# Delta rule in a hybrid decoder trunk: joining 16-row blocks by products with 32x32 weights instead of masked 128x128 weights

## The chip, the cores and the metric

The kernel runs on one NeuronCore of a Trainium2 chip. The metric is the device time of one execution in microseconds (us), as the median of several runs. A profile is one execution of its own; its times are counted from the start of its span.

## The reference

A decoder trunk of 4 layers works on 256 positions of 1024 channels, in fp32. Layers 0 and 3 mix the positions by attention, layer 1 by a short convolution, layer 2 by the gated delta rule; a convolutional feed-forward block follows each mixer. The change is in the delta rule alone:

```python
a_mat = jnp.where(strict, jnp.einsum('bhnid,bhnjd->bhnij', k_beta, k) * decay, 0.0)
t_mat = lax.linalg.triangular_solve(a_mat + eye, eye, left_side=True, lower=True, unit_diagonal=True)
u = t_mat @ v_beta
w = t_mat @ (k_beta * jnp.exp(gc)[..., None])
```

So for each of the 8 heads, and each chunk of the sequence, the inverse of a lower triangular matrix with unit diagonal is needed. The kernel takes chunks of 128 positions, so there are 16 such matrices of 128x128.

## The kernel before, in words

**The work.** Nearly all of the time is products of a stream of fp32 weights with the activations. Each weight tile is split into a high part `whi` (line 152, ScalarE) and a low part `wlo` (line 153, VectorE), and each product is three matmuls. The weights come in chunks of 8 tiles, each by one DMA. All matmuls are recorded at line 254, all transposes at 257.

**The delta rule.** `gdn` (layer 2) runs the weight products of queries, keys, values and gates as a *fill* in a fixed order (`GDN_FILL`), and weaves the delta rule's own small steps between them. The 8 heads form two halves of 4: half 0 (heads 0 to 3) and half 1 (heads 4 to 7). The fill brings half 0's queries and keys first, so half 0 goes through each step first, though half 1 stands first in the planner's list. A half has 8 matrices (4 heads, 2 chunks). Its steps, in `half`:

- `lengths` and `systems` make the matrices `aq` (line 758). `systems` sends them to DRAM (line 766) and, in the kernel before, makes `am` (line 772): `aq` times a mask of 1024 columns that keeps the 16x16 blocks which join two neighbouring diagonal blocks.
- `invert` reads the diagonal 16x16 blocks back (`bl`), inverts all of them on GpSimd in a loop of 14 steps with two operations each (lines 792 and 794), writes the result to DRAM and reads it back in another layout (`xc`, line 799). Line 802 spreads it over `xt32`, 256 columns, on VectorE; `turn` (line 809) transposes that in blocks of 32 into `xi32`.
- `join16` joins pairs of 16-blocks into inverses of 32x32: a product `pp` per matrix with `am` as weights, a masked copy `pm` (line 821, 1024 columns), a second product `pzt` with `pm` as weights, a sum (line 831), and `turn` again. Each product is 8 matmuls with 128x128 weights and 16 moving columns; an fp32 matmul shows as two instructions, so 16 instructions.
- `join_half` joins 32-blocks to 64 and 64-blocks to 128, in products with 32x32 and 64x64 weights (8 matmuls for each block and product).
- `solve` and `scores` apply the inverses to the values; values are transposed four matmuls at a time (line 257, `sm<-cs,u`).

In the trace `am`, `pm` and other tiles of the pool `big` show as `big`, `xi32` as `xi`, `xt32` as `xt`, a PSUM bank as `sm` (small steps, 4 banks) or `mm` (fill).

**What orders the work.** TensorE's instructions stand in program order, which a planner fixes while the program is built; the other engines are ordered by a scheduler. The planner (`Weave`) has a clock `t` of its own. Each fill step adds its cost: a pair of weight tiles, 6 matmuls, adds 2 x 0.327. After each fill step it goes through the list of steps:

```python
def pump(self):
    while True:
        step = next((s for s in self.steps if self.due(s[0]) <= self.t), None)
        ...
            cost, wait = next(step[1])
            self.t += cost
            step[0] = wait if isinstance(wait, tuple) else self.t + wait
```

So `yield 0.8, L_PM` says: this step took 0.8, and go on with it when 2.5 more have passed. The waits that matter are `L_BLOCKS` = 6.0 (blocks read back), `L_JOIN` = 13.0 (GpSimd's loop and the way through DRAM), `L_XI` = 1.0, `L_PM` = 2.5 and `LAG` = 1.75. A step that is placed too early is not wrong: TensorE waits for it on the chip, with everything behind it.

Of the kernel before, what the change touches and what calls it, by code (L numbers as in the profile page):

```python
# [9 lines left out]
F32 = mybir.dt.float32  # L10
# [5 lines left out]
P = 128  # L16
# [12 lines left out]
BLK = 16  # L29
# [12 lines left out]
L_QK, L_V, L_LEN, L_SYS, L_BLOCKS, L_JOIN, L_XI, L_PM, L_OUT = 6.0, 6.0, 1.0, 0.5, 6.0, 13.0, 1.0, 2.5, 1.0  # L42
# [15 lines left out]
C_TRI = C_BASE + 3 * P  # L58
C_NEG = C_TRI + P
C_BD = C_NEG + P  # L60
C_LV = C_BD + P
C_UP = C_LV + P
C_EO = C_UP + P
C_ST = C_EO + 2
C_N = C_ST + 2 * H


def constants():
    i = np.arange(P)
    c = np.zeros((P, C_N), np.float32)  # L70
    c[:, C_ID:C_ID + P] = np.eye(P)
    c[:, C_ONE:C_ONE + P] = 1.0
    dist0 = i[:, None] - i[None, :]
    dist1 = P + i[:, None] - np.arange(2 * P)[None, :]
    base = np.concatenate([dist0, dist1], 1).astype(np.float32)
    c[:, C_BASE:C_BASE + 3 * P] = np.where(base >= 0, base, 1e33)
    c[:, C_TRI:C_TRI + P] = i[:, None] <= i[None, :]
    c[:, C_NEG:C_NEG + P] = np.where(i[None, :] >= i[:, None], 0.0, -1e30)
    c[:, C_ST:C_ST + 2 * H] = i[:, None] % (2 * H) == np.arange(2 * H)[None, :]
    b = i // BLK  # L80
    c[:, C_BD:C_BD + P] = b[:, None] // 2 == b[None, :] // 2
    lower = (b[:, None] == b[None, :] + 1) & (b[:, None] % 2 == 1)
    c[:, C_LV:C_LV + P] = np.where(lower, -1.0, 0.0)
    c[:, C_UP:C_UP + P] = lower.T
    c[:, C_EO:C_EO + 2] = b[:, None] % 2 == np.arange(2)[None, :]
    return c


# [130 lines left out]
def trunk(ctx: ExitStack, tc: tile.TileContext, xT, wstream, pvec, cst, wba, hv, out):  # L219
    nc = tc.nc  # L220
    V, S, G = nc.vector, nc.scalar, nc.gpsimd
# [11 lines left out]
    cs = keep.tile([P, C_N], F32, name="cs")  # L233
# [25 lines left out]
    PE = Tensor()  # L259
# [3 lines left out]
    for _ in range(WARM):  # L263
        PE.matmul(psum.tile([P, 512], F32, name="sm", bufs=4)[:, :T], lhsT=idle[:, :P], rhs=idle,
                  start=True, stop=True)
# [10 lines left out]
    def bank(tag, bufs=4):  # L276
        return psum.tile([P, 512], F32, name=tag, bufs=bufs)
# [322 lines left out]
    def gdn(gain):  # L600
        nm = Norm()
        NS = 2 * G_H
        with tc.tile_pool(name="gdn", bufs=1) as pool, \
# [17 lines left out]
            def big(dt=F32):  # L621
                return pool.tile([P, NS, P], dt, name="big", bufs=NB)
# [4 lines left out]
            def gates():  # L627
# [12 lines left out]
                for t in range(2):  # L640
                    PE.matmul(pba[:, t * 16:(t + 1) * 16], lhsT=gs[:, t * P:(t + 1) * P],
                              rhs=cs[:4 * H, C_ST:C_ST + 2 * H], start=True, stop=True)
                for t in range(2):
# [101 lines left out]
            def systems(s):  # L745

                s.aq = pool.tile([P, NS, 2, P], F32, name="aq", bufs=2)
                yield 0, (f"d{s.h0}",)
                for a in range(G_H):
                    y = s.y[a]  # L750
                    pk = bank("sm")
                    for t in range(2):
                        ts = slice(t * P, (t + 1) * P)
                        PE.matmul(pk[:, t * T:(t + 1) * T], lhsT=y[:, 1, ts], rhs=y[:, 0:2, ts],
                                  start=True, stop=True)
                    for t in range(2):
                        m = 2 * a + t
                        V.scalar_tensor_tensor(s.aq[:, m], pk[:, t * T:(t + 1) * T].rearrange(
                            "p (q i) -> p q i", q=2), s.sk[:, m:m + 1],
                            s.dt[:, a, t, :].unsqueeze(1).to_broadcast([P, 2, P]), op0=ALU.mult, op1=ALU.mult)  # L760
                    yield 0.87, 0.5 * LAG

                nb = P // BLK
                row = (BLK * P + BLK) * nb
                d1 = dram.tile([NS * row], F32, name="d1")
                nc.sync.dma_start(
                    out=d1.rearrange("(m x) -> m x", m=NS)[:, :P * P].rearrange("m (p c) -> p m c", p=P),
                    in_=s.aq[:, :, 1, :])
                s.d1 = d1

                s.am = big()
                V.tensor_mul(s.am, s.aq[:, :, 1, :],
                             cs[:, C_UP:C_UP + P].unsqueeze(1).to_broadcast([P, NS, P]))

            def invert(s):

                nb, d1 = P // BLK, s.d1

                bl = pool.tile([NS * nb, BLK, BLK], F32, name="bl", bufs=1)
                with nc.allow_non_contiguous_dma(reason="16 values of a block's row"):  # L780
                    nc.sync.dma_start(
                        out=bl, in_=d1.rearrange("(q y) -> q y", q=NS * nb)[:, :BLK * P]
                        .rearrange("q (j c) -> q j c", j=BLK)[:, :, :BLK])
                xb = pool.tile([NS * nb, BLK, BLK], F32, name="xb", bufs=1)
                xm = pool.tile([NS * nb, BLK, BLK], F32, name="xm", bufs=1)
                G.memset(xb, 0.0)
                G.memset(xb.rearrange("p j i -> p (j i)")[:, ::BLK + 1], 1.0)
                yield 0, L_BLOCKS
                G.tensor_scalar(xb[:, 0, 1:], bl[:, 0, 1:], -1.0, None, op0=ALU.mult)
                for k in range(1, BLK - 1):  # L790
                    n, r = k + 1, BLK - 1 - k
                    G.tensor_mul(xm[:, :n, :r], xb[:, :n, k:k + 1].to_broadcast([NS * nb, n, r]),  # L792
                                 bl[:, k:k + 1, k + 1:].to_broadcast([NS * nb, n, r]))
                    G.tensor_sub(xb[:, :n, k + 1:], xb[:, :n, k + 1:], xm[:, :n, :r])  # L794
                d2 = dram.tile([NS, nb, BLK, BLK], F32, name="d2")
                nc.sync.dma_start(out=d2.rearrange("m b j i -> (m b) j i"), in_=xb)
                xc = pool.tile([P, NS, BLK], F32, name="xc", bufs=1)
                with nc.allow_non_contiguous_dma(reason="16 values of a block's row"):
                    nc.sync.dma_start(out=xc, in_=d2.rearrange("m b j i -> (b j) m i"))
                s.xt32 = pool.tile([P, NS, 2, BLK], F32, name="xt32", bufs=2)  # L800
                yield 0, L_JOIN
                after(V.tensor_mul(s.xt32, xc.unsqueeze(2).to_broadcast([P, NS, 2, BLK]),
                                   cs[:, C_EO:C_EO + 2].unsqueeze(1).unsqueeze(3).to_broadcast([P, NS, 2, BLK])))

# [5 lines left out]

            def join16(s):

                nb = P // BLK
                turn(s)
                yield 0, L_XI
                pp = bank("sm")
                for m in range(NS):
                    PE.matmul(pp[:, m * BLK:(m + 1) * BLK], lhsT=s.am[:, m, :], rhs=s.xi32[:, m, :BLK],
                              start=True, stop=True)
                pm = big()  # L820
                V.tensor_mul(pm.rearrange("p m (b i) -> p m b i", b=nb),
                             pp[:, :NS * BLK].rearrange("p (m i) -> p m i", m=NS).unsqueeze(2)
                             .to_broadcast([P, NS, nb, BLK]),
                             cs[:, C_LV:C_LV + P].rearrange("p (b i) -> p b i", b=nb).unsqueeze(1)
                             .to_broadcast([P, NS, nb, BLK]))
                yield 0.8, L_PM
                pzt = bank("sm")
                for m in range(NS):
                    PE.matmul(pzt[:, m * BLK:(m + 1) * BLK], lhsT=pm[:, m, :], rhs=s.xt32[:, m, 1, :],
                              start=True, stop=True)  # L830
                V.tensor_add(s.xt32[:, :, 1, :], s.xt32[:, :, 1, :],
                             pzt[:, :NS * BLK].rearrange("p (m i) -> p m i", m=NS))
                turn(s)
                yield 0.8, L_XI

                s.xt, s.xi = big(), pool.tile([P // 2, NS, P // 2], F32, name="xi", bufs=2)
                x32 = s.xt32.rearrange("p m e i -> p m (e i)")
                V.tensor_mul(s.xt.rearrange("p m (b i) -> p m b i", b=4),
                             x32.unsqueeze(2).to_broadcast([P, NS, 4, 2 * BLK]),
                             cs[:, C_BD:C_BD + P].rearrange("p (b i) -> p b i", b=4).unsqueeze(1)  # L840
                             .to_broadcast([P, NS, 4, 2 * BLK]))
                G.memset(s.xi, 0.0)
                for b in range(0, P // 2, 2 * BLK):
                    up = slice(b, b + 2 * BLK)
                    S.copy(s.xi[up, :, up], s.xi32[up])
# [291 lines left out]
```

## Time and profile before

| | |
|---|---|
| time, median of 3 runs | 1248.51 us (1247.18 to 1248.51) |
| the profiled execution's own time | 1247.2 us |
| its span, first to last instruction | 1245.1 us |
| mean granted TensorE clock | 0.994 |
| TensorE matmul, weight load | 1225.7 us (98%), 1127.5 us (91%) |
| VectorE, ScalarE, GpSimd | 982.9 (79%), 775.5 (62%), 104.4 us (8%) |
| DMA | 215.80 MB, mean 173 GB/s |

The delta rule's layer lies at about 550 to 790 us of the span. An engine's share is an average over the whole kernel; what the change can move is read in its own stage. A matmul's end is modelled, and matmuls overlap, so the distance between starts tells more of TensorE than the durations.

### The profile page before, as it was taken

Reading aid. Unit: us, or ns where it says so; the run is one execution under the profiler, and the core shown is the slowest. Engines: PE = TensorE matmul, PEld = TensorE weight load, DVE = VectorE, ACT = ScalarE, POOL = GpSimd, SP = SyncE. Lnnn points to the kernel's source line nnn. Section 1 sums busy time; section 2 is a strip of 40 time slices with the busy share of each in tenths; the row PEclk is TensorE's granted clock in tenths of the full one; section 3 lists DMA queues with packets and bytes.
Section 4 is the critical chain, followed back from the end, with each engine's and each line's share of the span. In section 5 each row is a group of like instructions: output and inputs, shape, how many; then the busy total and the mean of one; then the engine's idle time right before and its main releaser. Section 6 shows DMA issues by size and latency. Waiting matters only on the chain.

```text
span 1245.1 us, 22068 instructions
## 1 busy us (share of the span) xinstructions
PE 1225.7 (98%) x8366; PEld 1127.5 (91%) x8366; DVE 982.9 (79%) x1720; ACT 775.5 (62%) x1427; POOL 104.4 (8%) x147
## 2 busy tenths in 40 slices
PE   9999999999999999999997999999999999999997
PEld 8989988889999988889997999988889989988886
DVE  6756999966878999866995668999775756999952
ACT  6655777644445777645873666777554655777641
POOL 2002000001002000001045102000011002000000
PEclk9999999999999999999998999999999999999998
DMA  8544465655555465655344244555655444466650
GB/s 289 200 153 166 146 201 186 213 188 189 176 182 186 153 201 193 200 189 183 126 131 126 90 136 137 200 192 189 208 190 175 156 161 165 145 202 188 211 177 34
DMA packets 67418, 215.80 MB, mean 173 GB/s; under 512 B 11248, under 2 KB 14832, under 8 KB 67312
## 3 DMA queue, kind: packets, MB, share of 16 engines
q1 hardware_dynamic: 67024, 213.86, 52.3%
q8 instruction: 66, 1.08, 0.3%
q10 hardware_dynamic: 288, 0.52, 0.1%
q14 instruction: 40, 0.33, 0.1%
HBM read 212.13 MB, written 2.23 MB: 172 GB/s over the span
## 4 chain that ended last, share of the span: by engine, by line
PE 89%; DVE 4%; ACT 2%; DMA 2%; issue 1%; POOL 1%; SPq 0%; POOLq 0%; DVEq 0%; ACTq 0%
PE mm L254 72%; PE sm L254 16%; DVE wlo L153 2%; DMA wraw<-wstream 1%; PE sm L257 1%; DVE xl L292 1%; ACT whi L152 1%; DVE yqk L422 1%; POOL xb L794 1%; POOL xm L792 1%; ACT jk L729 0%; DMA bl<-d 0%; DVE x L392 0%; DVE big L692 0%; DMA xc<-d 0%
## 5 line engine op out<-in xcount | busy, mean ns | idle before, releaser
L153 DVE TENSOR_TENSOR wlo<-wraw,whi 128x1024 fp32r<-128x1024 f32 (+1 forms) x404 | 489.5, 1212 | 155.7 <-ACT whi L152 154.0
L152 ACT CAST whi<-wraw 128x1024 fp32r<-128x1024 f32 (+1 forms) x404 | 420.2, 1041 | 290.9 <-PE mm L254 239.5
L254 PE MATMUL mm<-xh,whi 128*128 128x256 f32 x1024 | 296.5, 290 | 0.2 <-ACT whi L152 0.2
L254 PE MATMUL mm<-xh,wlo 128*128 128x256 f32 x1024 | 289.1, 282 | 1.2 <-DVE wlo L153 1.2
L254 PE MATMUL mm<-xl,whi 128*128 128x256 f32 x1024 | 288.7, 282 | 0.7 <-DVE xl L292 0.7
L254 PE MATMUL mm<-xs,whi 128*128 128x512 f32 x704 | 248.3, 394 | 0.0
L254 PE MATMUL mm<-aw,whi 128*128 128x512 f32 x704 | 247.3, 393 | 0.0
L254 PE MATMUL mm<-aw,wlo 128*128 128x256 f32 x704 | 199.1, 283 | 0.0
L254 PE MATMUL mm<-xs,wlo 128*128 128x256 f32 x704 | 199.1, 283 | 0.0
L254 PEld LDWEIGHTS mm<-xh,wlo 128*128 128x128 f32 x1024 | 193.5, 189 | 2.3 <-DVE wlo L153 2.1
L254 PEld LDWEIGHTS mm<-xl,whi 128*128 128x128 f32 x1024 | 193.8, 189 | 1.8 <-DVE xl L292 1.1
L254 PEld LDWEIGHTS mm<-xh,whi 128*128 128x128 f32 x1024 | 193.7, 189 | 1.4 <-ACT whi L152 0.4
L254 PEld LDWEIGHTS mm<-aw,whi 128*128 128x128 f32 x704 | 132.2, 188 | 30.6
L254 PEld LDWEIGHTS mm<-xs,whi 128*128 128x128 f32 x704 | 132.2, 188 | 30.5
L422 DVE SCALAR_TENSOR_TENSOR y<-u,pv,y 128x255 f32<-128x255 f32 (+1 forms) x352 | 149.0, 478 | 0.4
L254 PE MATMUL sm<-xs,whi 128*128 128x512 f32 x384 | 135.7, 393 | 0.0
L306 POOL TENSOR_TENSOR sq<-sq 128x256 f32<-128x256 f32 x62 | 53.3, 859 | 974.6 <-ACT sq L304 972.8
L254 PEld LDWEIGHTS mm<-xs,wlo 128*128 128x128 f32 x704 | 132.4, 188 | 0.0
L254 PEld LDWEIGHTS mm<-aw,wlo 128*128 128x128 f32 x704 | 132.3, 188 | 0.0
L254 PE MATMUL sm<-xs,wlo 128*128 128x256 f32 x384 | 108.6, 283 | 0.0
L420 ACT ACTIVATE y<-u,pv 128x256 f32<-128x256 f32 x176 | 81.4, 504 | 11.9 <-DVE u L451 6.6
L254 PEld LDWEIGHTS sm<-xs,whi 128*128 128x128 f32 x384 | 72.1, 188 | 16.6
(210 smaller groups left out, 1509.5 us busy)
## 6 DMA issues: line engine op xcount, KB each, us to landing
wraw<-wstream SPq DMA_DIRECT2D x396, 512.0 KB, 3.4
wraw<-wstream SPq DMA_DIRECT2D x8, 256.0 KB, 4.8
x<-xT SPq DMA_DIRECT2D x8, 128.0 KB, 4.7
d<-aq SPq DMA_DIRECT2D x2, 512.0 KB, 3.7
out<-xg ACTq DMA_DIRECT2D x2, 256.0 KB, 2.5
cs<-cst SPq DMA_DIRECT2D x1, 329.0 KB, 6.4
pv<-pvec SPq DMA_DIRECT2D x1, 324.5 KB, 4.9
cs<-cst SPq DMA_DIRECT2D x1, 320.0 KB, 5.9
```

Source lines behind the costliest of these rows:

```text
L152: self.nc.scalar.copy(hi[:, s], raw[:, s])
L153: self.nc.vector.tensor_sub(lo[:, s], raw[:, s], hi[:, s].bitcast(F32))
L254: self.last = nc.tensor.matmul(*a, **k)
L257: self.last = nc.tensor.transpose(*a, **k)
L292: V.scalar_tensor_tensor(xl[n], xn, col(gain + n), xh[n].bitcast(F32), op0=ALU.mult, op1=ALU.subtract)
L306: G.tensor_add(sums[0], sums[0], sq)
L420: S.activation(y, u, AF.Copy, scale=col(taps[0]))
L422: V.scalar_tensor_tensor(y[:, d:], u[:, :T - d], col(c), y[:, d:], op0=ALU.mult, op1=ALU.add)
L792: G.tensor_mul(xm[:, :n, :r], xb[:, :n, k:k + 1].to_broadcast([NS * nb, n, r]), bl[:, k:k + 1, k + 1:].to_broadcast([NS * nb, n, r]))
L794: G.tensor_sub(xb[:, :n, k + 1:], xb[:, :n, k + 1:], xm[:, :n, :r])
```

## The change

`join16` no longer multiplies with 128x128 weights of which a mask has left some blocks. It takes each 32x32 diagonal block of the matrices by itself, as weights of 32x32 from `aq` in place, for 4 blocks and 8 matrices: 32 matmuls (64 instructions) per product instead of 8 (16 instructions). Within a block the mask of `pp` becomes a factor per row, 0 or -1 (`C_LO`), over 256 columns. `am` and its mask go, `pm` gets a tile of its own in place of one of the pool `big`, both PSUM banks are taken before the first product, and the constants that are loaded get 254 columns fewer. The planner's cost of each of the two products goes from 0.8 to 2.0.

```diff
-C_LV = C_BD + P
-C_UP = C_LV + P
-C_EO = C_UP + P
-C_ST = C_EO + 2
+C_EO = C_BD + P
+C_LO = C_EO + 2
+C_ST = C_LO + 2
...
-    lower = (b[:, None] == b[None, :] + 1) & (b[:, None] % 2 == 1)
-    c[:, C_LV:C_LV + P] = np.where(lower, -1.0, 0.0)
-    c[:, C_UP:C_UP + P] = lower.T
     c[:, C_EO:C_EO + 2] = b[:, None] % 2 == np.arange(2)[None, :]
+    c[:, C_LO] = np.where(b % 2 == 1, -1.0, 0.0)
...
-                s.am = big()
-                V.tensor_mul(s.am, s.aq[:, :, 1, :],
-                             cs[:, C_UP:C_UP + P].unsqueeze(1).to_broadcast([P, NS, P]))
...
             def join16(s):
 
-                nb = P // BLK
                 turn(s)
                 yield 0, L_XI
-                pp = bank("sm")
-                for m in range(NS):
-                    PE.matmul(pp[:, m * BLK:(m + 1) * BLK], lhsT=s.am[:, m, :], rhs=s.xi32[:, m, :BLK],
-                              start=True, stop=True)
-                pm = big()
-                V.tensor_mul(pm.rearrange("p m (b i) -> p m b i", b=nb),
-                             pp[:, :NS * BLK].rearrange("p (m i) -> p m i", m=NS).unsqueeze(2)
-                             .to_broadcast([P, NS, nb, BLK]),
-                             cs[:, C_LV:C_LV + P].rearrange("p (b i) -> p b i", b=nb).unsqueeze(1)
-                             .to_broadcast([P, NS, nb, BLK]))
-                yield 0.8, L_PM
-                pzt = bank("sm")
-                for m in range(NS):
-                    PE.matmul(pzt[:, m * BLK:(m + 1) * BLK], lhsT=pm[:, m, :], rhs=s.xt32[:, m, 1, :],
-                              start=True, stop=True)
+                pp, pzt = bank("sm"), bank("sm")
+                blocks = [slice(b, b + 2 * BLK) for b in range(0, P, 2 * BLK)]
+
+                for b in blocks:
+                    for m in range(NS):
+                        PE.matmul(pp[b, m * BLK:(m + 1) * BLK], lhsT=s.aq[b, m, 1, b], rhs=s.xi32[b, m, :BLK],
+                                  start=True, stop=True)
+                pm = pool.tile([P, NS, 2, BLK], F32, name="pm", bufs=1)
+                V.tensor_mul(pm, pp[:, :NS * BLK].rearrange("p (m i) -> p m i", m=NS).unsqueeze(2)
+                             .to_broadcast([P, NS, 2, BLK]),
+                             cs[:, C_LO:C_LO + 2].unsqueeze(1).unsqueeze(3).to_broadcast([P, NS, 2, BLK]))
+                yield 2.0, L_PM
+                for b in blocks:
+                    for m in range(NS):
+                        PE.matmul(pzt[b, m * BLK:(m + 1) * BLK], lhsT=pm[b, m].rearrange("p e i -> p (e i)"),
+                                  rhs=s.xt32[b, m, 1, :], start=True, stop=True)
                 V.tensor_add(s.xt32[:, :, 1, :], s.xt32[:, :, 1, :],
                              pzt[:, :NS * BLK].rearrange("p (m i) -> p m i", m=NS))
                 turn(s)
-                yield 0.8, L_XI
+                yield 2.0, L_XI
```

## Rows read from the trace of the kernel before

**Rows 1.** The page's busy time, share of the span and instructions, by engine.

```profile
PE 1225.7 (98%) x8366; PEld 1127.5 (91%) x8366; DVE 982.9 (79%) x1720; ACT 775.5 (62%) x1427; POOL 104.4 (8%) x147
```

**Rows 2.** TensorE's waits over the span: us in total, times, longest.

```profile
PE sm L254 <- DVE xi L809: 5.7, 2, 5.1
```

**Rows 3.** Stretches around the first product: length, busy by engine, granted clock, DMA.

```profile
620.00:632.00 12.00, 10.67 (x80) 9.80 (x79) 11.45 (x26) 11.06 (x47) 3.44 (x2) 1.00 0.62 203
...
664.20:667.60 3.40, 3.40 (x17) 3.40 (x17) 1.81 (x3) 0.00 (x0) 0.00 (x0) 0.50 1.03 390
667.60:670.50 2.90, 2.90 (x14) 2.90 (x15) 2.36 (x2) 0.00 (x0) 0.00 (x0) 0.50 0.30 91
670.50:674.00 3.50, 3.50 (x32) 3.50 (x32) 0.95 (x3) 1.86 (x3) 1.56 (x7) 0.99 0.73 169
```

**Rows 4.** Timeline of TensorE, half 0's products: start, us busy, shape, count, idle before.

```profile
664.18 3.57 PE L254 MATMUL sm<-xi,big 128*128 128x16 f32 x16 [5.09 <-DVE xi L809]
667.59 0.56 PE L254 MATMUL mm<-xh,whi 128*128 128x256 f32 x1
...
671.85 1.86 PE L254 MATMUL sm<-xt,big 128*128 128x16 f32 x16
```

**Rows 5.** Timeline of TensorE, half 0's later joins to half 1's first product.

```profile
675.79 1.07 PE L254 MATMUL sm<-xi,aq 32*32 32x32 f32 x32 [0.58 <-DVE xi L809]
...
681.04 0.69 PE L254 MATMUL sm<-xt,m 32*32 32x32 f32 x16 [0.84 <-ACT big L866]
...
688.83 0.39 PE L254 MATMUL mm<-xh,whi 128*128 128x256 f32 x1
...
691.07 1.06 PE L254 MATMUL sm<-big 128*128 128x128 f32 x8
691.96 0.60 PE L257 MATMUL sm<-cs,u 128*128 128x128 f32 x4
692.32 0.36 PE L254 MATMUL mm<-xh,whi 128*128 128x256 f32 x1
...
693.82 1.85 PE L254 MATMUL sm<-xi,big 128*128 128x16 f32 x16
```

**Rows 6.** Timeline of VectorE, 635 to 693 us.

```profile
635.17 1.21 DVE L772 TENSOR_TENSOR big<-aq,cs 128x1024 f32<-128x1024 f32 x1
...
645.07 1.30 DVE L153 TENSOR_TENSOR wlo<-wraw,whi 128x1024 fp32r<-128x1024 f32 x1
...
663.59 0.45 DVE L809 STREAM_TRANSPOSE xi<-xt 128x256 f32<-128x256 f32 x1
663.96 0.83 DVE L758 SCALAR_TENSOR_TENSOR aq<-sm,sk,big 128x256 f32<-128x256 f32 x2
664.82 1.23 DVE L772 TENSOR_TENSOR big<-aq,cs 128x1024 f32<-128x1024 f32 x1
667.78 1.23 DVE L821 TENSOR_TENSOR big<-sm,cs 128x1024 f32<-128x1024 f32 x1 [1.74 <-PE sm L254]
...
692.09 0.42 DVE L802 TENSOR_TENSOR xt<-xc,cs 128x256 f32<-128x256 f32 x1 [2.03 <-DMA xc<-d]
692.54 0.45 DVE L809 STREAM_TRANSPOSE xi<-xt 128x256 f32<-128x256 f32 x1
```

**Rows 7.** Timeline of GpSimd, from the loops of the two halves.

```profile
645.36 1.15 POOL L792 TENSOR_TENSOR xm<-xb,bl 64x55 f32<-64x55 f32 x1
646.59 0.30 POOL L794 TENSOR_TENSOR xb<-xb,xm 64x55 f32<-64x55 f32 x1
...
684.85 1.21 POOL L794 TENSOR_TENSOR xb<-xb,xm 64x15 f32<-64x15 f32 x1
```

**Rows 8.** Timeline of the DMA issues: `aq` of each half to DRAM.

```profile
634.68 0.38 SPq L766 DMA_DIRECT2D d<-aq  x1
...
664.82 0.38 SPq L766 DMA_DIRECT2D d<-aq  x1
```

## The prediction

> **What bounds the kernel.** I read the shares by engine first, then TensorE's waits, then the chain through the delta rule, then the other engines there. TensorE is busy 98% of the span and VectorE 79% [rows 1], so VectorE time saved is worth nothing by itself: only TensorE work, or a wait of TensorE, moves the end. The waits are few, and the largest by far stands in the changed function: 5.7 us in two waits for `xi` of line 809, one of them 5.1 [rows 2]. There the first product of half 0 (heads 0 to 3, the half that comes first) stands at the head of TensorE's queue until 664.18 [rows 4]. Behind it the granted clock is 0.50 (the 1.2 GHz level) till about 670.5, against 1.00 (2.4 GHz) before, also in a stretch with waits of about 1 us each [rows 3]. What is awaited is no VectorE work: GpSimd's 28 loop operations per half, then two DMAs through DRAM, then lines 802 and 809 [rows 7, 8, 6].
>
> Half 1 runs the same chain later, and there is no wait: VectorE finishes `xi` at 692.54 + 0.45 = 692.99, and TensorE, still at the work put in front, comes to the product at 693.82 [rows 6, 5]. The margin is 0.8 us. This margin decides the change.
>
> **The order of TensorE.** It is fixed by the planner's clock, in its own units. I set 0 at half 0's first 16-block product. A pair of fill products (6 matmuls) costs 0.654, and a step goes ahead at the first point at which it is due. *Before*, by the code: product to 0.8; due at 3.3, so 4 pairs, 3.416; second product, 4.216; 2 pairs, 5.524; join of 32 (1.4), 6.924. Half 1, due at 6.0 after its `L_BLOCKS`, goes on here: `L_JOIN` ends at 19.924. Then 3 pairs, 8.886; join (2.1) and a transpose (0.22), 11.206; 3 pairs, 13.168; join of 64, 14.568; 3 pairs, 16.53; its second step, 17.93; 3 pairs, 19.892. Half 1 misses its due time by 0.03; half 0's solve (0.87), 20.762; half 1's `xt32` and turn are placed, due in 1.0; transposes 0.22; 2 pairs, 22.29; half 1's first product. The trace has this order: 18 matmuls, solve, transposes, 12 matmuls, product [rows 5].
>
> *After*, with 2.0 for 0.8: 2.0; 4 pairs, 4.616; 6.616, where half 1 goes on (`L_JOIN` ends at 19.616); 2 pairs, 7.924; 9.324; 3 pairs, 11.286; 13.386 and transposes 13.606; 3 pairs, 15.568; 16.968; 3 pairs, 18.93; second step of the join of 64, 20.33. Half 1 is now due: turn placed, due 21.33; 2 pairs, 21.638; half 1's first product. So there are 17 pairs between the two first products instead of 20, and the solve and the second transposes slip behind. The costs claim 2.0 for a product that the trace has at 1.85 [rows 5], so the planner believes 2.4 more has passed than the chain of GpSimd and DMAs, which knows nothing of these costs, has gained.
>
> **The change part by part.**
>
> *The late join.* Between the end of half 0's join of 64 (688.83) and the product (693.82) lie 4.99 us [rows 5]. Two pairs remain in front: 12 matmuls, 1.50 us by the row from 692.32 to 693.82 [rows 5], and about 0.04 to change tile size. TensorE arrives at 690.37, and with the longer products of half 0 (below) at about 690.8. `xi` lets it start 0.14 after its end, as it did for half 0 (663.59 + 0.45 to 664.18) [rows 4, 6]: 693.13. So a wait of 2.3 us, and the work behind it is done 693.13 - 690.37 = 2.76 us later than now. The 3 pairs, solve and transposes that went behind are not lost, only moved: +2.8. The lengthening of half 0's products vanishes in this wait.
>
> *The products.* Sixteen instructions of 128x128 weights are busy for 1.85 us [rows 5]. After, there are 64 of 32x32 (each fp32 matmul shows as two instructions). The join of 32 shows that shape with 32 moving columns: 32 instructions are busy for 1.07 us, 16 for 0.69 [rows 5]; so 0.024 each and 0.31 fixed gives 1.83, twice the first gives 2.14. I take 2.05, nearer the upper: +0.2. Below, if the 16 moving columns instead of 32 set the pace, half of the upper: 1.07, or -0.8; above, +0.3. At half clock half 0's first one doubles like the row of now (3.57 us) [rows 4], inside the wait. Only half 1's two products count: 2 x 0.2 = +0.4 (-1.6 to +0.6).
>
> By the Trainium skill (TensorE: Matmul & The Clock Gate, Part 3) 32x32 tiles at distinct array positions run concurrently, and a matmul with 32 rows alone costs what one with 128 does. The loop runs 16 instructions on one position before the next, and the rows of 32x32 agree with no fourfold gain.
>
> *The masks.* `am` (line 772, 1.22 us) goes and `pm` (1.23 us, 1024 columns) shrinks to 256; the nearest row, line 802, has 256 columns in 0.42 [rows 6]. That is 1.2 + 0.8 us of VectorE per half. `am` of half 1 stands in front of no one: VectorE idles 1.74 us before the product's result [rows 6]. `pm` is hidden by the 4 pairs behind the product (4.26 us, 667.59 to 671.85) [rows 4]; without that cover it would give 0.8 per half. `am` of half 0 (635.17) leaves after the DMA of `aq` is issued (634.68) [rows 6, 8], so the chain doesn't see it. All at 0. The extra PSUM bank held from the first to the second product costs 0: solve and transpose take the other two, and 3 pairs follow. The smaller `cst` load is one among some 400 transfers: 0.
>
> *Sum.* 2.8 + 0.4 = +3.2 us on the profiled execution's 1247.2 (span 1245.1 and 2.1 around it): 1250.4. The median of the runs is 1248.51, 1.3 above that execution; so 1251.7.
>
> **The rivals.** What a measurement can tell from no change is about 0.2%, 2.5 us.
>
> *The join is in time.* Half 1's chain begins when line 758 has written the last `aq` (663.96 and 664.82), and these stand on VectorE behind line 802, which waits for half 0's DMA [rows 6, 8]. VectorE's order is the scheduler's; if with `am` gone it puts 758 first, the chain starts some 6 us sooner and the wait disappears. Against it: 802 was put first while 758 still waited for TensorE, and the change touches neither. Left is 4 x 0.2: 1249.3, no change that can be told. Chance 0.20.
>
> *The clock falls as well.* The wait of 5.1 us was followed by 6.3 us at half clock, a loss of 3.1; the stretch with 1 us waits kept 1.00 [rows 3, 4]. A wait of 2.3 lies between, nearer the short ones. If it falls: +6.3, 1254.8. Chance 0.12.
>
> *Faster: GpSimd undisturbed.* Beside a 1024-column operation of line 153 a GpSimd operation of half 0's loop took 1.15 us instead of about 0.3 [rows 7]. I count 5 stretched ones in half 0's loop (some 4.0 us in all) and 4 in half 1's (3.5). The end is set by half 1's `xi`, so each of them lost is worth its price. `am` gone shifts VectorE by 1.2, and could free some. From 5.7 us on, about 7 of the 9, the kernel is faster by over 0.2%. With all, `xi` is there at 685.6, and TensorE, 4.0 sooner at its first product, arrives at 686.8 and sets the end: 3.2 - 6.3 = -3.1, 1245.4. Against it: line 153 comes as often as before, and VectorE is back to back there. Chance 0.08. The Trainium skill (GPSIMD Engine Reference, 1. Specifications) has GpSimd share its SBUF interfaces with VectorE instructions of two SBUF inputs; this row agrees.
>
> *Tiles side by side.* If the four blocks overlap, a product takes some 0.5 us, 1.3 less: 2.8 - 2.6 = +0.2, 1248.7. The blocks change position only every 16 instructions. Chance 0.04.
>
> **How the numbers follow.** The late join by itself has 0.56. Its own range is +0.5 to +5: 2.8 with the products' bounds gives 1.2 to 3.4, and one GpSimd operation more or less stretched in either half (0.8 each) the rest: 1249.0 to 1253.5. A quarter of it (0.14) lies under 2.5 us. So slower 0.42 + 0.12 = 0.54, same 0.14 + 0.20 + 0.04 = 0.38, faster 0.08. The range leaves out the faster case and what lies above the fallen clock: 1247.5 to 1255.0.
>
> **What would show it.** TensorE has 192 matmuls more (48 in each of four products), in groups of 64 busy for 1.8 to 2.1 us at the full clock. Line 772 is gone and two operations of 256 columns at 0.4 to 0.5 stand for line 821. The waits for `xi` of line 809 get a second large one of about 2.3 us before half 1's first product, with 12 matmuls between it and the join of 64, and half 0's solve behind it. The granted clock stays 1.00 there. Wrong it would be if TensorE arrives no earlier than `xi`, if half 1's `aq` goes to DRAM before half 0's `xt32`, or if the 64 small instructions take well under 1.8 us.

## The result, and the profile after

The changed kernel takes 1255.3 us (median of 4 runs, 1254.22 to 1256.2), the kernel before beside it 1248.35 us (4 runs, 1247.18 to 1248.51): 1.0054 times as long, interval 1.004 to 1.0068. It is slower by 7.0 us, where 3.2 were forecast. The profiled execution has a span of 1253.4 us against 1245.1, so 8.3 are to be found, and a mean clock of 0.988.

The page's busy time by engine:

```profile
PE 1231.1 (98%) x8558; PEld 1132.7 (90%) x8558; DVE 979.0 (78%) x1718; ACT 774.0 (62%) x1427; POOL 104.7 (8%) x147
```

There are 192 matmul instructions more (two for each fp32 matmul, so 96 matmuls, where the prediction has "192 matmuls"), and two VectorE instructions fewer. TensorE is busy for 5.4 us more than in [rows 1], though the new products take hardly longer than the old ones (below): some of its work ran slowly. TensorE's waits (total, times, longest):

```profile
PE sm L251 <- DVE xi L802: 8.9, 2, 4.6
...
PE sm L254 <- DVE m L924: 0.8, 1, 0.8
```

Line 802 is now the turn that writes `xi`, line 251 the matmuls, 254 the transposes. The first row answers [rows 2]: the wait of half 0 is still there, and a second one nearly as long has come. The other row is new. TensorE's timeline from half 0's first product on, which answers [rows 4, 5]:

```profile
663.01 3.00 PE L251 MATMUL sm<-xi,aq 32*32 32x16 f32 x64 [4.59 <-DVE xi L802]
...
693.09 3.00 PE L251 MATMUL sm<-xi,aq 32*32 32x16 f32 x64 [4.28 <-DVE xi L802]
696.02 2.08 PE L251 MATMUL sm<-big 128*128 128x128 f32 x8
697.89 1.06 PE L254 MATMUL sm<-cs,u 128*128 128x128 f32 x4
...
701.01 1.89 PE L251 MATMUL sm<-xt,pm 32*32 32x16 f32 x64
...
712.29 0.94 PE L254 MATMUL sm<-cs,m 128*128 128x128 f32 x4 [0.85 <-DVE m L924]
...
715.72 1.21 PE L251 MATMUL sm<-xi,aq 64*64 64x64 f32 x16
```

The order is the one that the planner's clock gave: half 1's first product now stands in front of half 0's solve (`big` x8) and transposes. Compare the two groups `xt,pm` and `xi,aq` of 64: 1.89 at the full clock, 3.00 behind a wait. The solve behind the second wait takes 1.87 from start to start, against 0.89 in [rows 5]. The granted clock of the stretches (last column but two) says why:

```profile
674.00:688.00 14.00, 13.96 (x185) 13.10 (x185) 9.46 (x17) 9.84 (x20) 9.36 (x23) 1.00 0.17 56
...
693.00:696.50 3.50, 3.41 (x66) 3.40 (x67) 0.37 (x1) 0.00 (x0) 0.00 (x0) 0.50 0.42 154
696.50:699.50 3.00, 3.00 (x18) 3.00 (x18) 0.05 (x1) 1.04 (x3) 0.00 (x0) 0.61 0.00 0
699.50:702.00 2.50, 2.50 (x51) 2.37 (x50) 1.32 (x2) 2.39 (x6) 0.00 (x0) 1.00 0.00 0
...
712.00:716.00 4.00, 3.71 (x19) 3.52 (x20) 0.14 (x1) 1.57 (x4) 0.00 (x0) 0.57 0.01 4
```

So there are two new stretches at the 1.2 GHz level, one behind the second wait for `xi`, one behind the wait of 0.85 for `m`. VectorE, where [rows 6] had lines 802 and 809 back to back:

```profile
691.03 0.42 DVE L795 TENSOR_TENSOR xt<-xc,cs 128x256 f32<-128x256 f32 x1 [3.97 <-DMA xc<-d]
691.37 1.22 DVE L150 TENSOR_TENSOR wlo<-wraw,whi 128x1024 fp32r<-128x1024 f32 x1
692.50 0.44 DVE L802 STREAM_TRANSPOSE xi<-xt 128x256 f32<-128x256 f32 x1
696.13 0.42 DVE L816 TENSOR_TENSOR pm<-sm,cs 128x256 f32<-128x256 f32 x1 [3.18 <-PE sm L251]
```

The data came 1.06 us earlier than before (691.03 against 692.09), but a `wlo` of 1.22 us now stands between the two steps, so `xi` is ready at 692.94, practically as before (692.99). `pm` takes 0.42.

### The profile page after: what moved, and what is told of

It reads as the page before. It is cut to its first block, busy times and chain, and to the rows that moved or that the text cites. A ratio compares the mean times of both kernels' runs of the same rounds, so it can differ in the third digit from the quotient of the medians.

```text
span 1253.4 us, 22450 instructions
## 1 busy us (share of the span) xinstructions
PE 1231.1 (98%) x8558; PEld 1132.7 (90%) x8558; DVE 979.0 (78%) x1718; ACT 774.0 (62%) x1427; POOL 104.7 (8%) x147
```

## The experiments

### The change with the old costs in the planner, and the old kernel with the new ones

```diff
-                yield 2.0, L_PM
+                yield 0.8, L_PM
...
-                yield 2.0, L_XI
+                yield 0.8, L_XI
```

> The changed kernel with the planner's old cost of 0.8 for each of the two products, so that half 1's first product stands behind 20 pairs, the solve and the transposes again. Theory 'order' (the cost of 2.0 brings half 1's first product forward, and all of the loss follows from that): the wait there shrinks from 4.3 us to under 1.5, the second and third stretch at half clock vanish, and the time is 1246.5 to 1249.5 us, no slower than the kernel before. Rival 'small tiles' (64 instructions of 32x32 in place of 16 of 128x128 cost the time by themselves, through the clock or the issue): the order hardly matters and the time stays at 1253 us or more.

1248.7 us against 1247.9 for the kernel before beside it, ratio 1.0005 (0.9994 to 1.0017; the range is the 95% interval, here and below). TensorE at the two first products, and the clock from behind half 0's product on:

```profile
663.11 3.00 PE L251 MATMUL sm<-xi,aq 32*32 32x16 f32 x64 [4.68 <-DVE xi L802]
...
692.42 1.87 PE L251 MATMUL sm<-xi,aq 32*32 32x16 f32 x64 [0.91 <-DVE xi L802]
```

```profile
670.00:715.00 45.00, 43.44 (x645) 41.28 (x643) 25.82 (x49) 28.09 (x66) 14.58 (x31) 1.00 0.25 76
```

The small products and masks stay, the loss is gone. The reverse, `before` with 2.0 in both places:

> The kernel before, masks and 128x128 products as they were, with the planner's cost of 2.0 for each of the two products. Theory 'order': TensorE comes to half 1's first product at about 690.4 us of the span, its xi at 693.0, a wait of about 2.6 us where there was none; +2.8 us if the clock holds, +5 if it falls there: 1251 to 1254. Rival 'small tiles': 1248 to 1249, as before.

1252.69 us, ratio 1.004 (1.0027 to 1.0054). The large products, with the new order alone, are slower. In this execution the clock fell earlier, behind a wait of 0.8 for half 0's join to 64, so TensorE came late to the product and its wait for `xi` was only 0.22; but the wait for `m` (line 931 here) is there, with its half clock:

```profile
692.30 1.93 PE L254 MATMUL sm<-xi,big 128*128 128x16 f32 x16 [0.22 <-DVE xi L809]
...
708.74 0.86 PE L257 MATMUL sm<-cs,m 128*128 128x128 f32 x4 [0.85 <-DVE m L931]
```

```profile
681.00:687.00 6.00, 5.96 (x55) 5.71 (x55) 1.45 (x2) 2.96 (x7) 2.28 (x10) 0.72 0.25 70
...
709.00:713.00 4.00, 4.00 (x29) 3.78 (x28) 0.00 (x0) 1.65 (x3) 0.00 (x0) 0.57 0.00 0
```

So the two edits of one number carry the loss: without them nothing is lost that can be told, and alone they cost 4.8 us of the 7.0 (the two intervals overlap). The rest of the change is neutral.

### Does the small shape itself lose the clock?

Extra products that nobody reads, in `before`, behind half 0's last join, where TensorE doesn't wait: 256 instructions of 32x32 with 16 columns, then in two other kernels 64 of 128x128 with 16 columns, and 58 of 128x128 with 256 columns.

```diff
+                if n == 64 and s.h0 == 0:
+                    idle_bank = bank("sm")
+                    for _ in range(4):
+                        for b in range(0, P, 32):
+                            for m in range(NS):
+                                r = slice(b, b + 32)
+                                PE.matmul(idle_bank[r, m * BLK:(m + 1) * BLK], lhsT=s.aq[r, m, 1, r],
+                                          rhs=s.xi32[r, m, :BLK], start=True, stop=True)
```

> The kernel before with 256 more instructions (128 matmuls) of 32x32 weights and 16 columns on TensorE right behind half 0's last join, where it has run at full clock for 15 us and waits for nothing; their result isn't used, and the planner is told nothing of them. If small tiles don't hold the clock: the granted clock falls to 0.50 during or right behind these about 7 us, though TensorE is never idle. If only waits let it fall: it stays 1.00. The time is 1248 plus 7 to 13 either way.

> As the run with 256 small instructions, but with 64 instructions (32 matmuls) of 128x128 weights and 16 columns, about as long (6.8 us) at the same place. If small tiles are what loses the clock: it stays at 1.00 here. If any product with 16 columns loses it, or a change of the order of the other engines does: it falls here too.

> The kernel before with 58 more matmuls of 128x128 weights and 256 columns (6.9 us, result not used) behind half 0's last join, where 256 narrow and 64 wide instructions with 16 columns let the clock fall. If it is the few columns that lose the clock: 1.00 throughout here, and the time is 1248 + 7 = 1255. If more work of any sort at this place does: 0.50 here too, 1260.

One execution each: 1258.08, 1261.65 and 1257.16 us. The extra group of each, and stretches over it with the clock, first 32x32:

```profile
690.10 7.90 PE L254 MATMUL sm<-xi,aq 32*32 32x16 f32 x256
```

```profile
693.00:697.00 4.00, 4.00 (x133) 4.00 (x131) 0.00 (x0) 0.00 (x0) 0.00 (x0) 0.75 0.26 101
```

128x128 with 16 columns:

```profile
689.78 12.11 PE L254 MATMUL sm<-xi,aq 128*128 128x16 f32 x64
```

```profile
691.00:693.00 2.00, 2.00 (x15) 2.00 (x14) 0.78 (x3) 0.00 (x0) 0.00 (x0) 0.68 0.51 170
693.00:697.00 4.00, 4.00 (x20) 4.00 (x21) 0.00 (x0) 0.00 (x0) 0.00 (x0) 0.50 0.17 69
```

And with 256 columns:

```profile
692.10 7.22 PE L254 MATMUL sm<-xh 128*128 128x256 f32 x58
```

```profile
693.00:697.00 4.00, 4.00 (x35) 4.00 (x34) 1.10 (x3) 0.33 (x1) 0.00 (x0) 1.00 0.37 131
```

TensorE was busy in all of these stretches. Both groups with 16 columns ended at 0.50 (32x32: 0.50 in 697 to 701), that with 256 columns stayed at 1.00. So, in one execution each, 32x32 isn't what loses the clock. The changed kernel has only 64 such instructions in a row, 1.9 us; whether these do it is for the next experiment.

### What is the second stretch at half clock worth, and what brings it?

Matmuls with 256 columns that nobody reads, in front of half 1's first product in the changed kernel: 30, and 54.

```diff
+                if s.h0 == G_H:
+                    spare = bank("sm")
+                    for _ in range(30):
+                        PE.matmul(spare[:, :T], lhsT=xh[0][:, :P], rhs=xh[1], start=True, stop=True)
```

> The changed kernel with 30 more matmuls of 128x128 weights and 256 columns (about 3.6 us, result not used) right in front of half 1's first product, where TensorE waits 4.3 us. If the wait's length alone costs (theory 'late join' without the clock): they fit into the wait, nothing is gained or lost, 1255 us. If the half clock behind that wait is part of the price: the wait shrinks to about 0.7 us, the clock stays at 1.00 behind it, and the first product, the solve and the transposes take 1.8, 0.9 and 0.35 us instead of 2.9, 1.9 and 0.7: about 2.4 us faster in spite of more work, 1252 to 1253.5.

> Leaves nothing out and adds work that nobody reads: 54 matmuls with 256 columns in front of half 1's first product in the changed kernel, some 6.8 us by the pace of the 30 (3.76 us), so that TensorE comes to the product later than xi is ready (693.5 + 0.4 with 30 added) and nothing is left of the wait. Theory (the clock falls behind the wait, and costs about 2.5 us by itself): the wait is under 0.3, the product starts at about 694.8, which is 1.7 later than in the changed kernel, its 64 instructions take 1.9 us and not 2.9, the clock stays 1.00, and the time is 1255.3 + 1.7 - 2.5 = 1254.5, or about 1251.8 if the half clock at 712 to 716 doesn't come either. Rival (products with 16 columns lose the clock here by themselves, whatever stands in front): 2.9 us at a clock of 0.5 in 695 to 700 and about 1257.

With 30: 1254.7 us, ratio 1.005 (1.0037 to 1.0062).

```profile
687.96 3.76 PE L251 MATMUL sm<-xh 128*128 128x256 f32 x30
693.99 2.93 PE L251 MATMUL sm<-xi,aq 32*32 32x16 f32 x64 [2.26 <-DVE xi L802]
696.85 2.08 PE L251 MATMUL sm<-big 128*128 128x128 f32 x8
```

`xi` came 0.9 later as well, so 2.26 us of wait were left where 0.7 were expected. Product and solve take about their half-clock times all the same (the first product starts 8.44 before the second, 7.92 in the changed kernel). It is by chance the length of wait that the prediction had.

With 54: 1255.13 us, ratio 1.0052 (1.0039 to 1.0065).

```profile
688.02 6.64 PE L251 MATMUL sm<-xh 128*128 128x256 f32 x54
694.59 1.89 PE L251 MATMUL sm<-xi,aq 32*32 32x16 f32 x64
696.42 1.16 PE L251 MATMUL sm<-big 128*128 128x128 f32 x8
...
700.07 1.89 PE L251 MATMUL sm<-xt,pm 32*32 32x16 f32 x64
...
711.35 0.96 PE L254 MATMUL sm<-cs,m 128*128 128x128 f32 x4 [0.85 <-DVE m L928]
```

Now there is no wait, and the 64 products keep the full clock (it is 1.00 in every stretch from 688 to 711). So at this product the wait brings the half clock, not the shape. Its price: the first product starts 1.50 later than in the changed kernel (694.59 against 693.09), the second 0.94 earlier (700.07 against 701.01), hence 2.44 us. Of this 1.50 is spent again on the later start; the span is shorter by 1.0, as that leaves. The medians (1255.13 and 1255.3) are too coarse to show it. The wait for `m` and its half clock stay.

### Putting half 1's first product back, with the costs of 2.0

```diff
-                yield 0, L_JOIN
+                yield 0, L_JOIN + (3.5 if s.h0 else 0)
```

> The changed kernel with its cost of 2.0, but half 1 goes on 3.5 later on the planner's clock than L_JOIN says. TensorE then has the order of the kernel before between the two first products (18 matmuls, solve, transposes, 12 matmuls). Theory (the whole loss is that half 1's first product comes before its xi): no wait over 1 us there, one wait of about 5 for xi in half 0 alone, no half clock after 675, and 1248 to 1249.5, which can't be told from the kernel before. Rival (the cost of 2.0 does its harm elsewhere too, in the order of the steps behind, as the wait of 0.85 for m at 712): 1251 to 1254 with the wait at the first product gone.

1248.88 us, ratio 1.0005 (0.9994 to 1.0016).

```profile
690.19 0.60 PE L254 MATMUL sm<-cs,u 128*128 128x128 f32 x4
...
692.13 1.89 PE L251 MATMUL sm<-xi,aq 32*32 32x16 f32 x64
...
708.07 0.60 PE L254 MATMUL sm<-cs,m 128*128 128x128 f32 x4
```

Solve and transposes stand in front again, nothing waits for `xi` in half 1, nor for `m` at 708, and the clock is 1.00 from 675 to 750. The theory holds, the rival (harm of the costs elsewhere) doesn't: with the product back in its place the wait for `m` is gone too.

The same in the kernel with costs of 0.8, with 1.5 later, to take up the 0.91 left there:

> The changed kernel with the old cost of 0.8, and half 1 goes on 1.5 later than L_JOIN says, which puts one pair more (6 matmuls, 0.75 us) in front of half 1's first product and takes up the wait of 0.91 that stood there with the cost of 0.8 alone. Theory (what is left of the change with the cost of 0.8 is this wait): the wait falls to about 0.2, and the time by 0.7 from 1248.7 to 1248.0, within 0.2% of the kernel before. Rival (the wait is hidden, since a later wait for VectorE sets the end): 1248.7 as with the cost of 0.8 alone.

1248.46 us, ratio 1.0005 (0.9995 to 1.0014): no difference that can be told from 1248.7. The expected short wait missed: it was 1.20, at 694.23, since `xi` was turned at 693.64 (691.84 with 0.8 alone). The chain's data were 1.3 later, and VectorE put `u` (0.68) between the two steps.

### Attacking the first wait: `L_JOIN` longer for both halves

`L_JOIN` 20.0 instead of 13.0, in the changed kernel with costs of 0.8 and in the kernel before:

> The changed kernel with the planner's cost of 0.8 and L_JOIN = 20 instead of 13: 9 more pairs of fill stand in front of half 0's first product, and half 1's keeps its distance. Theory 'order' (what a product costs here is what TensorE waits for, and the clock behind a wait): the wait of 4.6 us and the half clock of 8 us behind it go, 1248 - 4.6 - 3 = 1240 us, if half 1's xi isn't waited for then (TensorE arrives at about 691, xi at 692: up to 1.5 us back). Rival: the fill that is moved ahead is missing later, and the time stays at 1248.

> The kernel before with L_JOIN = 20. Theory 'order': the same gain as with the small products, 1240 us within 1.5. If the small products and the VectorE work they save are worth something once nothing waits: the changed kernel with L_JOIN = 20 is over 1 us faster than this one.

1256.13 us (ratio 1.0063, 1.0049 to 1.0077) and 1257.39 (1.0068, 1.0053 to 1.0084); the two can't be told apart. The wait isn't removed, only moved 7 us on. TensorE and VectorE of the first:

```profile
669.90 3.00 PE L251 MATMUL sm<-xi,aq 32*32 32x16 f32 x64 [5.60 <-DVE xi L802]
```

```profile
664.34 1.23 DVE L150 TENSOR_TENSOR wlo<-wraw,whi 128x1024 fp32r<-128x1024 f32 x1 [0.84 <-ACT whi L149]
665.48 2.45 DVE L419 SCALAR_TENSOR_TENSOR u<-u,pv 128x255 f32<-128x255 f32 x6
667.85 0.42 DVE L795 TENSOR_TENSOR xt<-xc,cs 128x256 f32<-128x256 f32 x1
```

The scheduler put `xt32` behind the split of later weights and behind `u`, the work of the fill that now comes first. The data were there: line 795 waits for nothing.

A wait that is only moved doesn't explain 8 us more. The rest is late in the layer, where TensorE is busy without a break in the kernel before (40.00 of 40 us in 720 to 760), and waits twice here, with 6.3 us at half clock behind:

```profile
747.24 0.66 PE L254 MATMUL sm<-cs,m 128*128 128x128 f32 x4 [1.96 <-DVE m L924]
750.01 1.31 PE L251 MATMUL mm<-big,whi 128*128 128x256 f32 x2 [2.11 <-ACT big L412]
```

The same two waits stand in the trace of the other kernel. It fits the rival, that the fill moved ahead is missing later; no run shows that by itself.

### Does half 1's chain start earlier if VectorE makes its `aq` first?

The kernel with 3.5 for half 1 (above), and half 0 later by 2.5 or 4.0. VectorE then does all of half 1's `aq` before half 0's `xt32`.

```diff
-                yield 0, L_JOIN + (3.5 if s.h0 else 0)
+                yield 0, L_JOIN + (3.5 if s.h0 else 2.5)
```

> The changed kernel, cost 2.0, half 1 3.5 later as before and half 0 2.5 later: 24 instead of 12 matmuls stand in front of half 0's first product (1.5 us more work), and VectorE's order now has half 1's last aq in front of half 0's xt32, so that half 1's chain starts about 6 us sooner; between the two first products TensorE has the order of the kernel before. Theory (a wait for xi costs what it lasts, and its half clock beside it): the wait of 4.6 in half 0 falls to about 3.1, the half clock stays, half 1 has no wait, and the time is 1248.9 - 1.5 = 1247.4. Rival (half 1's transfer of aq, now beside half 0's xc, or VectorE's new order makes half 0's xi later by as much): 1248.9 or more.

> As the run with half 0 2.5 later, but half 0 4.0 later. TensorE then has the changed kernel's own order around half 1's first product (join of 64, 12 matmuls, product, and only then the solve and transposes), while half 1's chain has started about 6 us sooner, so its xi should be there at about 686. Theory (the changed kernel's loss is only that xi comes later than the product): no wait over 0.5 at half 1's product, clock 1.00 there, and with 36 instead of 12 matmuls in front of half 0's product (3.0 us more work) a wait of 2 to 2.5 there and about 1246.5. Rival A (the order of steps itself costs, by the wait of 0.85 for m and the solve behind): 1249 to 1251. Rival B (VectorE's wlo, which now stands in front of half 0's xt32, waits for ScalarE and TensorE, as with 7.0 more in both halves): half 0's wait is over 4 again, some us later, and 1252 or more.

1254.44 us (ratio 1.0042, 1.003 to 1.0054) and 1252.78 (1.0031, 1.002 to 1.0042): both theories failed. `aq` was complete at 658.62 with 2.5. SyncE's queue there:

```profile
659.56 0.38 SPq L792 DMA_DIRECT2D xc<-d  x1
660.03 1.62 SPq L127 DMA_DIRECT2D wraw<-wstream  x3
661.70 0.42 SPq L763 DMA_DIRECT2D d<-aq  x1
...
670.18 0.63 SPq L774 DMA_DIRECT2D bl<-d  x1
```

`aq` goes out at 661.70, behind half 0's `xc` and three loads of weights, and its transfer takes 8.5 us to land (4.4 in the run with 3.5 alone), so that the blocks are read back at 670.18, later than the 667.99 of that run. The chain is not earlier at all. (The DMA share is 0.98 to 1.01 from 661.7 to 668 in both runs; why one transfer took longer isn't shown.) With 2.5 the wait for `xi` in half 0 fell as expected (3.04), but one of 2.03 for the second turn and one of 2.5 for `m` came, each with half clock behind it. With 4.0 VectorE put a `wlo`, which waited 4.5 for ScalarE, in front of half 0's `xt32` (the expectation's rival B, though half 0's wait stayed under 4), and half 1's first product waits again:

```profile
665.43 3.00 PE L251 MATMUL sm<-xi,aq 32*32 32x16 f32 x64 [3.34 <-DVE xi L802]
...
694.29 1.87 PE L251 MATMUL sm<-xi,aq 32*32 32x16 f32 x64 [3.18 <-DVE xi L802]
```

Behind this wait of 3.18 the product itself kept the full clock (1.87); it fell only then, and the solve took 2.08:

```profile
696.00:698.00 2.00, 2.00 (x15) 1.97 (x12) 0.82 (x3) 0.00 (x0) 0.00 (x0) 0.53 0.28 109
```

No kernel here beats the one before by anything that can be told.

## Why the prediction was wrong in size and right in kind

**The order of TensorE** came out as worked out, to the pair, and with it the margin of 0.8 us in front of half 1's product was lost, as foretold.

**The late join.** The forecast was a product at 693.13, done 2.76 later than before. It started at 693.09. The work that went behind it is 3 pairs (2.25 us by [rows 5], 12 matmuls in 1.50), solve (0.89) and transposes (0.36), 3.5 in all; less the 0.73 by which the product starts earlier than 693.82, that is +2.8. This term was right. The wait was longer (4.28 for 2.3), since TensorE came 2.0 sooner: half 0's product began 1.17 earlier, and the waits of 0.58 and 0.84 in its later joins [rows 5] were gone, here and in the runs with the old costs. That gain the prediction had not seen ("all at 0"); it lies in front of `xi` and is worth nothing there.

**The products.** 64 instructions are busy for 1.89 us (2.05 foretold, 1.85 before), and 1.83 lie from start to start, against 1.70 before: +0.12 per product, so +0.2 for half 1's two, not +0.4.

**The step that failed** is "the granted clock stays 1.00 there". The wait of 2.3 was put "nearer the short ones", and the rival in which the clock falls got a chance of 0.12. It fell: 0.50 in 693 to 696.5. At the foretold length it falls too, as the run with 2.26 shows in its one profile. Its price by the run with 54 matmuls is 2.4 us; the rival had taken 3.1 from half 0. With it alone the sum is 2.8 + 0.2 + 2.4 = 5.4, about 1253.8 and inside the stated range; what took the time above it, and above the rival's 1254.8, is a term that the prediction did not have.

**What no case had,** that missing term, is the second consequence of the order, the transposes of `m` that now follow the solve with no fill between: 0.85 of wait and, in this execution, half clock from 712 to 716, where the stretch from these transposes to the next join takes 3.43 us instead of 1.95 (712.29 to 715.72, against 708.07 to 710.02 with the product put back, both with 12 matmuls between). That is 0.85 + 1.48 = 2.3.

**The sum** for the profiled executions: 2.8 + 0.2 + 2.4 + 2.3 = 7.7 of 8.3. What is left, 0.6, isn't assigned. The time from the start of half 1's first product to the span's end shows the same in each run (the first three have the order of before around it, the others the new one; half clock that came before the product isn't in it):

| kernel | product starts | span | from product to end | half clock behind `xi`, wait for `m`, half clock behind that |
|---|---|---|---|---|
| before | 693.82 | 1245.1 | 551.3 | none |
| costs 0.8 | 692.42 | 1244.8 | 552.4 | none |
| half 1 later by 3.5 | 692.13 | 1243.6 | 551.5 | none |
| after | 693.09 | 1253.4 | 560.3 | all three |
| 30 matmuls more | 693.99 | 1252.8 | 558.8 | first two |
| 54 matmuls more | 694.59 | 1252.4 | 557.8 | last two |
| before with costs 2.0 | 692.30 | 1249.6 | 557.3 | last two |

To the new order, with 3.5 us of work more behind the product, belong 551.3 + 3.5 + 0.2 = 555.0 (554.8 with the large products). Half clock behind `xi` costs 2.4 in the changed kernel and 8.44 - 5.48 = 3.0 in the run with 30, where 5.48 is the way from first to second product in the run with 54; the wait for `m` is 0.85, the half clock behind it 1.5 (1.4 with the large products). So the last four come to 559.8, 558.8, 557.4 and 557.0, which is 0 to 0.5 under the measured ones. The first three, with none of these losses, differ by up to 1.1 among themselves, so this remainder can't be told from nothing.

**The rivals.** *The join is in time:* no, and its mechanism is wrong. With VectorE's `aq` first, half 1's chain started no earlier; `aq` was issued behind other transfers in SyncE's queue and took 8.5 us to land. *GpSimd undisturbed:* no; four operations of each half's loop take over 1 us, as before. *Tiles side by side:* no, 1.83 us from the group's start to the next is 28.6 ns for each of its 64 instructions. The Trainium skill (TensorE: Matmul & The Clock Gate, Part 1) has starts of matmuls never closer than about 25 ns, however few the columns; this average agrees, but single starts in the trace of the changed kernel don't. On one 32x32 position they mostly lie 30 to 33 ns apart (the group at 701.01); at each change of position three of them follow the one before by only 5 to 6 ns. The blocks do overlap, but only there.

**Left open.** That the new order without any wait would cost next to nothing is the table's arithmetic; no run had that order with `xi` early, since both attempts to make it early failed. Nor is it settled why the half clock behind the wait for `m` came with 54 matmuls and not with 30, where the wait was as long (0.85 and 0.86).

## What to carry to other kernels

Where a planner weaves small steps into a stream by costs that are written down, a new cost is a change of its own: here it carried the whole loss, and the new instructions none, so run it apart from them. Work out the order that it gives and look for the step whose margin to an asynchronous chain is smallest. Price a long wait of TensorE at its length plus the half clock behind it (in this layer every wait of 2.03 us or more had some behind it, in every trace kept; one of 1.75 in the run with 4.0 had none, those of about 0.85 now and then), and look at what the moved steps run into next.

## What the runs showed of the hardware that was not expected

- TensorE lost its full clock while it was busy without a pause: in 128x128 products with 16 columns the granted clock was 0.68 in 691 to 693 and 0.50 behind that; in 32x32 ones it was 0.75 in 693 to 697 and 0.50 in 697 to 701 (one execution each). Beside products with 256 columns it stayed at 1.00. The Trainium skill (TensorE: Matmul & The Clock Gate, Part 1) ties the fall to an idle engine; these runs show one that by the profile was not idle.
- At half clock the 32x32 products take 45.8 ns from start to start on average (2.93 us for 64) against 28.6 at the full one, 1.6 times; the 128x128 solve doubles (1.87 against 0.89).
- The clock doesn't fall at a fixed point of a wait: behind 4.28 us the product already ran at half clock, behind 3.04 and 3.18 (half 0 later by 2.5, by 4.0) it still ran at the full one, and the clock fell after it.
- The same short wait doesn't always do the same: behind half 0's wait of 0.8 for ScalarE's `big` the clock stayed at 1.00 in the execution of before (674 to 688), and fell to a mean of 0.72 to 0.74 in 681 to 687 in four executions with that same wait (the kernel before with costs of 2.0, and the three with extra products).
